# First norm from feature tiles summed on GpSimd, first projection tiles evacuated unscaled, memory norm moved into the key projection

## The chip, the cores and the metric

One core of a Trainium2 chip runs the whole kernel. The metric is the device time in microseconds of one execution; a run's median over several executions is compared. The engines are named as in the profile: PE (TensorE matmul), PEld (its weight load), DVE (VectorE), ACT (ScalarE), POOL (GpSimd), SP (SyncE, which here only issues DMAs).

## The reference

A decoder trunk of two layers on 256 positions of 2048 features, with 256 memory tokens. Only its beginning matters here:

```
mem_n = rms_norm(mem, norm_mem)
hn = rms_norm(h, norm_mix[0])            # y = x * rsqrt(mean(x*x) + eps) * g
z = hn @ w_in                            # (256 x 2048) @ (2048 x 4096)
gate_b, gate_c, xa, u = split(z)         # u: the last 1024 columns, input of the S5 branch
ya = gate_b * causal_dwconv(gate_c * xa, conv_w)
ys = s5_branch(u, ...)                   # a scan over positions
h = h + concat(ya, ys) @ w_out
# then, in each layer: cross attention into mem_n
k, v = split(mem_n @ w_kv, 2)            # w_kv of each of the two layers
```

Behind it come cross attention, a gated MLP with a short convolution, a layer with sliding-window attention, again cross attention and MLP, and a final norm.

## The kernel before

Features lie on the 128 partitions and the 256 positions along the free dimension, so an activation is 16 tiles (`KT`) of 128 x 256. All products are float32 in three passes: operand and weight are each split into a rounded high part and the rest. `split_gain` does it for an activation, with the norm's gain on the way: ACT writes the high part (L67) and DVE the rest (L68). `wload` does it for a weight block: SP issues its DMA into one of three `raw` buffers (L82), ACT writes `hi` (L90), DVE writes `lo` (L91); `hi` and `lo` have four buffers of 128 x 1024 each, two weight tiles' worth. `mm_hi` multiplies `hi` with both parts of the operand (128 x 512 moving columns at once at L105, or two times 256 at L102 and L103 with `one=True`), `mm_lo` multiplies `lo` with the high part (L110). `add_halves` adds the two halves of a PSUM bank (ACT copy L160, DVE add L161). PSUM has two pools of four banks each, `pp` (for `gemm`) and `pm` (`bank()`).

A norm's factor depends on the position alone, so it can be applied after the product. In later layers its sums come from `stat_add` on each new residual tile: ACT squares the tile (L174), POOL adds the squares up (L172); `stat_col` sums over partitions with a one-column matmul (L186), `rsqrt_col` takes the inverse root with an initial guess and three Newton steps on DVE, and `stat_bc` spreads it over partitions with a diagonal matrix (L225) and a matmul (L227) as `rbc`.

The first norm is done in another way. `even_mixer` starts with the eight weight tiles of `u`, numbers 24 to 31 of `ev_w_in`. `first_tiles` computes tiles 0 to 3 of them together while x and the weights arrive in pieces, k-tile by k-tile. `tok_col` loads x a second time with the positions on the partitions (`x_tok`, two DMAs on ACT's queue, released by a copy that waits for `h[10]`), and one ACT square for each half, with its sum along the row (L201), gives the column of sums. Tiles 4 and 5 go to banks of the pool `pm`; the broadcast is issued behind tile 4. Then the memory's sums are taken in the same way from `mem_tok`, and `memT` is loaded with the features on the partitions. Only then are tiles 0 to 5 evacuated by `evac_u`, which multiplies with `rbc`. `gemm` does tiles 6 and 7, with half of the sixteen `split_gain` of the memory behind each. Last come the memory's broadcast and `load_consts`, nine small constant loads on SP.

`x_tok`, `mem_tok`, `memT` and the states of S5's odd groups take turns in one buffer (tag `S`, one slot).

`mem_kv` then computes keys (`xa_k`, 16 tiles) and values (`xa_v`) of the memory for both layers; `after`, called behind each tile, takes steps of the generator `s5`, so that the S5 branch (DVE, ACT, a few matmuls) is spread over this time. The gates' 24 tiles follow, and the output projection. A key is stored unscaled, and scaled with the memory's broadcast when the cross attention loads it; a value is scaled with the column `mcol` when it is evacuated.

The order of each engine's queue is fixed when the kernel is built: a planner orders the instructions by its own costs, with the program's order as priority, so that later work is put into what it takes for gaps (S5's exponential, `vexp`, L347 and on, is an example). On the chip each queue is then followed in that order.

## Time and profile before

| | us |
|---|---|
| median of 3 runs | 2846.25 |
| lowest and highest | 2845.36, 2848.18 |
| the profiled execution | 2847.27 |
| its span, first to last instruction | 2845.5 |
| PE busy in the span | 2805.7 |
| DVE, ACT, POOL busy | 1952.9, 1566.1, 345.4 |

The profile is of one execution; its span is 1.8 us shorter than its time. All times inside it are counted from the span's start. PE's row says 99% busy, as an average over the whole kernel: the page's slices show the first of 40 at 7 tenths and nearly all others at 9 or more. A timeline row gives start, duration, engine, line, operation, out<-in, shapes, count, and in brackets the idle time of its engine before it and what ended it.

### The profile page before, as it was taken

What the parts mean: (1) busy time and instruction counts of PE and PEld (TensorE: products, weight loads), DVE (VectorE), ACT (ScalarE), POOL (GpSimd) and SP (SyncE); (2) the same over time, 40 slices, a digit from 0 to 9 for tenths busy, and PEclk for the clock granted to TensorE, in tenths of its full rate; (3) what the DMA queues carried; (4) which work ended last, traced back from release to release, by engine and by line L of the source; (5) the groups of instructions that cost most, each with busy time, mean ns of one, the idle gap of its engine ahead of it and who ended that gap; (6) DMA issues with size and microseconds to landing.
All of it is one profiled execution on the core that took longest, in us unless ns stands there. A gap on an engine that the chain in (4) does not pass through costs nothing.

```text
span 2845.5 us, 43900 instructions
## 1 busy us (share of the span) xinstructions
PE 2805.7 (99%) x17155; PEld 2492.1 (88%) x17155; DVE 1952.9 (69%) x3171; ACT 1566.1 (55%) x2509; POOL 345.4 (12%) x382
## 2 busy tenths in 40 slices
PE   7999999999999999999999999999999999999998
PEld 6988989998998888888888888889888888888887
DVE  5878697866766666666666778776666666666666
ACT  5766766644654544545545566655555455454454
POOL 0000000001001311202102310000122012021121
PEclk8999999999999999999999999999999999999999
DMA  7555555555555545555455554455455454654544
GB/s 283 204 201 189 206 191 205 210 179 181 206 188 182 189 171 210 184 185 197 170 207 184 179 193 154 154 208 185 165 188 195 165 207 171 213 189 166 208 170 142
DMA packets 90081, 538.83 MB, mean 189 GB/s; under 512 B 10672, under 2 KB 17168, under 8 KB 38672
## 3 DMA queue, kind: packets, MB, share of 16 engines
q1 hardware_dynamic: 86080, 520.47, 52.1%
q10 hardware_dynamic: 3792, 15.55, 1.4%
q8 instruction: 134, 2.20, 0.3%
q14 instruction: 75, 0.61, 0.1%
HBM read 525.45 MB, written 10.53 MB: 188 GB/s over the span
## 4 chain that ended last, share of the span: by engine, by line
PE 93%; DVE 3%; DMA 2%; ACT 1%; issue 1%; SPq 0%; POOL 0%; DVEq 0%; ACTq 0%; POOLq 0%
PE ps L105 49%; PE ps L110 28%; PE ps L102 3%; PE ps L103 3%; PE ps L326 2%; PE ps L327 2%; PE ps L331 2%; DVE lo L91 1%; PE m L856 1%; DMA raw<-in_ev_u 1%; PE m L762 1%; ACT stmp L496 1%; ACT hi L90 0%; DMA s5p<-in_s5p 0%; PE m L748 0%
## 5 line engine op out<-in xcount | busy, mean ns | idle before, releaser
L91 DVE TENSOR_TENSOR lo<-raw,hi 128x1024 fp32r<-128x1024 f32 (+2 forms) x1033 | 1202.2, 1185 | 414.4 <-ACT hi L90 161.6
L105 PE MATMUL ps<-op,hi 128*128 128x512 f32 x6069 | 1466.6, 392 | 6.5 <-DVE rcol L212 5.4
L90 ACT CAST hi<-raw 128x1024 fp32r<-128x1024 f32 (+2 forms) x1033 | 1002.1, 983 | 825.1 <-PE ps L105 695.1
L105 PEld LDWEIGHTS ps<-op,hi 128*128 128x128 f32 x6069 | 1114.3, 189 | 225.5 <-ACT hi L90 5.6
L110 PEld LDWEIGHTS ps<-op,lo 128*128 128x128 f32 x6976 | 897.4, 191 | 37.8 <-DVE lo L91 6.1
L110 PE MATMUL ps<-op,lo 128*128 128x256 f32 x6976 | 918.2, 283 | 4.8 <-DVE lo L91 4.8
L102 PE MATMUL ps<-op,hi 128*128 128x256 f32 x907 | 223.2, 286 | 6.2 <-ACT hi L90 6.1
L172 POOL TENSOR_TENSOR acc<-acc,t 128x256 f32<-128x256 f32 x84 | 77.0, 917 | 1229.1 <-ACT t L174 1229.1
L103 PE MATMUL ps<-op,hi 128*128 128x256 f32 x907 | 221.5, 284 | 0.0
L102 PEld LDWEIGHTS ps<-op,hi 128*128 128x128 f32 x907 | 174.8, 193 | 9.4 <-ACT hi L90 7.8
L103 PEld LDWEIGHTS ps<-op,hi 128*128 128x128 f32 x907 | 174.9, 193 | 0.1
L160 ACT COPY t<-ps 128x256 f32<-128x256 f32 x232 | 85.9, 371 | 150.6 <-PE ps L110 149.7
L893 POOL TENSOR_TENSOR t<-t,rbc 128x256 f32<-128x256 f32 x88 | 68.8, 781 | 749.1 <-DVE t L161 721.2
L896 DVE SCALAR_TENSOR_TENSOR t<-t,ff_conv 128x255 f32<-128x255 f32 x88 | 43.0, 488 | 141.8 <-ACT t L895 141.8
L899 POOL TENSOR_TENSOR t<-t,rbc 128x256 f32<-128x256 f32 x88 | 109.2, 1241 | 216.4 <-ACT t L898 216.4
L496 ACT ACTIVATE stmp<-S,s_pw 128x256 f32<-128x256 f32 (+3 forms) x256 | 118.0, 525 | 27.7 <-DVE S L503 24.1
L68 DVE SCALAR_TENSOR_TENSOR op<-h,gains,op 128x256 fp32r<-128x256 f32 x96 | 67.8, 713 | 86.6 <-ACT op L67 86.4
L75 DVE TENSOR_TENSOR op<-t,op 128x256 fp32r<-128x256 f32 x104 | 43.9, 425 | 116.8 <-ACT op L74 116.7
L326 PE MATMUL ps<-hi,op 128*128 128x512 f32 x256 | 101.2, 395 | 2.2 <-ACT hi L90 2.1
L327 PE MATMUL ps<-hi,op 128*128 128x512 f32 x256 | 99.9, 390 | 0.0
L161 DVE TENSOR_TENSOR t<-ps,t 128x256 f32<-128x256 f32 x232 | 96.4, 416 | 0.0
L905 POOL TENSOR_TENSOR t<-t 128x256 f32<-128x256 f32 x88 | 67.0, 762 | 135.0 <-DVE t L161 134.7
(219 smaller groups left out, 1727.9 us busy)
## 6 DMA issues: line engine op xcount, KB each, us to landing
raw<-in_ff_gate SPq DMA_DIRECT2D x88, 1024.0 KB, 4.8
raw<-in_ff_up SPq DMA_DIRECT2D x88, 1024.0 KB, 4.8
raw<-in_ff_down SPq DMA_DIRECT2D x128, 704.0 KB, 4.0
raw<-in_xa_k SPq DMA_DIRECT2D x32, 1024.0 KB, 5.1
raw<-in_xa_v SPq DMA_DIRECT2D x32, 1024.0 KB, 4.9
raw<-in_xa_q SPq DMA_DIRECT2D x32, 1024.0 KB, 4.8
raw<-in_xa_o SPq DMA_DIRECT2D x32, 1024.0 KB, 4.8
raw<-in_ev_w_in SPq DMA_DIRECT2D x28, 1024.0 KB, 4.9
```

The costliest lines, as they stand in the source:

```text
L90: nc.scalar.copy(hi, s)
L91: nc.vector.tensor_tensor(lo, s, hi.bitcast(F32), op=ALU.subtract)
L102: nc.tensor.matmul(ps[:, :T], lhsT=hi, rhs=o[:, :T], start=k == 0, stop=False)
L103: nc.tensor.matmul(ps[:, :T], lhsT=hi, rhs=o[:, T:], start=False, stop=False)
L105: nc.tensor.matmul(ps, lhsT=hi, rhs=o, start=k == 0, stop=False)
L110: self.nc.tensor.matmul(ps[:, :T], lhsT=w[k][1], rhs=ops[k][:, :T], start=False, stop=k == K - 1)
L160: self.nc.scalar.copy(t, ps[:, T:])
L161: self.nc.vector.tensor_tensor(out, ps[:, :T], t, op=ALU.add)
L326: nc.tensor.matmul(ps[b], lhsT=o[:, b * P:(b + 1) * P], rhs=w[j][0], start=k == 0, stop=False)
L327: nc.tensor.matmul(ps[b], lhsT=o[:, T + b * P:T + (b + 1) * P], rhs=w[j][0], start=False, stop=False)
L496: nc.scalar.activation(tmp[:, x, :, p - p0, :], at(0, both, p), AF.Copy, scale=pw[:, x, k, 8 * b + p:8 * b + p + 1])
L899: nc.gpsimd.tensor_tensor(y, y, self.rbc, op=ALU.mult)
```

## The change

- `tok_col` and the input `x_tok` go. `first_tiles` calls `stat_begin`, and `stat_add` on each k-tile of x, four k-tiles behind its split; `stat_col` follows behind tile 4 and `stat_bc` behind tile 5.
- Tiles 0 to 3 are evacuated at once and unscaled into their `u` buffers; tiles 4 to 7 all go through `gemm` and the pool `pp`, and are evacuated unscaled. `scale_u` multiplies the `u` tiles with `rbc` in place, six of them behind tile 5 and the others each behind its own tile.
- `memT` is loaded on SP's queue, one half behind tile 4 and one behind tile 5; the memory's splits stay behind tiles 6 and 7.
- The memory's norm moves into the first layer's key projection: `mem_tok` is loaded on SP behind key tile 2, its halves are squared behind tiles 5 and 6, `rsqrt_col` and `load_consts` follow behind tile 8, the broadcast behind tile 10.

```diff
@@ -188,19 +188,6 @@
                 nc.tensor.matmul(ps[:, b:b + 1], lhsT=self.sq[:, c], rhs=self.ones[:, :1], start=False, stop=True)
         return self.rsqrt_col(ps[:, :2], tag)
 
-    def tok_col(self, src, S, tag, behind=None):
-
-
-        nc = self.nc
-        if behind is not None:
-            nc.scalar.copy(S[:, :, 0], behind)
-        ss = self.smp.tile([P, 2], F32, name="ss", tag="ss")
-        for b in range(2):
-            nc.scalar.dma_start(S[:, b, :], src[:, b, :])
-        for b in range(2):
-            nc.scalar.activation(S[:, b, :], S[:, b, :], AF.Square, accum_out=ss[:, b:b + 1])
-        return self.rsqrt_col(ss, tag)
-
     def rsqrt_col(self, ms, tag):
         nc = self.nc
         v = self.smp.tile([P, 2], F32, name="v", tag="rs_v")
@@ -258,18 +245,24 @@
     def first_tiles(self, load_x, xs):
 
         ps = [self.pp.tile([P, 512], F32, name="ps", tag="ps") for _ in range(4)]
+        self.stat_begin()
+        lag = 4
         k = 0
         for step in (1, 1, 2, 2, 2, 4, 4):
             load_x(k, k + step)
             w = self.wload(self.I["ev_u0"][:, k:k + step, :], step, 512)
             for j in range(step):
                 xs.append(self.split_gain(self.h[k + j], self.gain(G_MIX, k + j)))
+                if k + j >= lag:
+                    self.stat_add(self.h[k + j - lag])
                 for n in range(4):
                     self.nc.tensor.matmul(ps[n], lhsT=w[j][0][:, n * P:(n + 1) * P], rhs=xs[k + j], start=k + j == 0, stop=False)
             for j in range(step):
                 for n in range(4):
                     self.nc.tensor.matmul(ps[n][:, :T], lhsT=w[j][1][:, n * P:(n + 1) * P], rhs=xs[k + j][:, :T], start=False, stop=k + j == KT - 1)
             k += step
+        for k in range(KT - lag, KT):
+            self.stat_add(self.h[k])
         return ps
 
     def load_consts(self):
@@ -302,7 +295,7 @@
         return evac, nxt
 
 
-    def mem_kv(self, l, kvp, after):
+    def mem_kv(self, l, kvp, after_k, after):
         nc = self.nc
         kv = self.dp.tile([4, P, 2048], F32, name=f"kv{l}")
         cur = {}
@@ -314,7 +307,7 @@
             nc.scalar.copy(cur["k"][:, n % 4, :], ps[:, :T])
             if n % 4 == 3:
                 nc.scalar.dma_start(kv[n // 4][:, :1024], cur["k"].rearrange("p a b -> p (a b)"))
-        self.gemm(lambda n: self.I["xa_k"][l, n], range(16), self.memop, KT, evac, after=after, one=True)
+        self.gemm(lambda n: self.I["xa_k"][l, n], range(16), self.memop, KT, evac, after=after_k, one=True)
         for c in range(4):
             ps = [self.pp.tile([P, 512], F32, name="ps", tag="ps") for _ in range(2)]
             for q in range(4):
@@ -552,36 +545,65 @@
             u, ya, ys = [], [], []
 
             def evac_u(n, ps):
-                z = self.t1()
-                self.add_halves(z, ps)
+
                 w = pool.tile([P, T], F32, name=f"u{n}", tag=f"u{n}")
-                nc.vector.tensor_tensor(w, z, rbc, op=ALU.mult)
+                self.add_halves(w, ps)
                 u.append(w)
+
+            def scale_u(ns):
+                for n in ns:
+                    nc.vector.tensor_tensor(u[n], u[n], rbc, op=ALU.mult)
+            place = lambda shape: pool.tile(shape, F32, name="S", tag="S")
             ps = self.first_tiles(load_x, xs)
-            place = lambda shape: pool.tile(shape, F32, name="S", tag="S")
-            self.tok_col(self.I["x_tok"], place([P, 2, D]), "h", self.h[10][:, :2])
-            for n in range(4, 6):
-                ps.append(self.bank())
-                self.mm(ps[n], self.wload(win(24 + n), KT, P), xs, 0, KT, KT)
+            for n in range(4):
+                evac_u(n, ps[n])
+            mem = place([P, KT, T])
+
+            def load_mem(c):
+                nc.sync.dma_start(mem[:, 8 * c:8 * c + 8, :], self.I["memT"][:, 8 * c:8 * c + 8, :])
+            self.memop = []
+
+            def mem_step(k0, k1):
+                for k in range(k0, k1):
+                    self.memop.append(self.split_gain(mem[:, k, :], self.gain(G_MEM, k)))
+
+            def after_u(n):
+                nonlocal rbc
                 if n == 4:
+                    self.stat_col()
+                    load_mem(0)
+                elif n == 5:
                     rbc, _ = self.stat_bc()
+                    load_mem(1)
+                    scale_u(range(0, 6))
+                elif n == 6:
+                    mem_step(0, 8)
+                    scale_u((6,))
+                else:
+                    scale_u((7,))
+                    mem_step(8, 16)
+            rbc = None
+            self.gemm(lambda n: win(24 + n), range(4, 8), xs, KT, evac_u, after=after_u)
             r2 = self.smp.tile([P, T], F32, name="r2", tag="r2", bufs=1)
             nc.vector.tensor_tensor(r2, rbc, rbc, op=ALU.mult)
-            self.mcol = self.tok_col(self.I["mem_tok"], place([P, 2, D]), "mem")
-            mem = place([P, KT, T])
-            for c in range(2):
-                nc.scalar.dma_start(mem[:, 8 * c:8 * c + 8, :], self.I["memT"][:, 8 * c:8 * c + 8, :])
-            for n in range(6):
-                evac_u(n, ps[n])
-            self.memop = []
-
-            def mem_step(i):
-                for k in range(8 * i, 8 * (i + 1)):
-                    self.memop.append(self.split_gain(mem[:, k, :], self.gain(G_MEM, k)))
-            self.gemm(lambda n: win(24 + n), range(6, 8), xs, KT, evac_u, after=lambda n: mem_step(n - 6))
-            self.rcol = self.mcol
-            self.mrbc, _ = self.stat_bc("mem")
-            self.load_consts()
+
+
+            mt = {}
+
+            def mem_norm(n):
+                if n == 2:
+                    mt["S"] = place([P, 2, D])
+                    mt["ss"] = self.smp.tile([P, 2], F32, name="ss", tag="ss")
+                    for b in range(2):
+                        nc.sync.dma_start(mt["S"][:, b, :], self.I["mem_tok"][:, b, :])
+                elif n in (5, 6):
+                    b = n - 5
+                    nc.scalar.activation(mt["S"][:, b, :], mt["S"][:, b, :], AF.Square, accum_out=mt["ss"][:, b:b + 1])
+                elif n == 8:
+                    self.mcol = self.rsqrt_col(mt["ss"], "mem")
+                    self.load_consts()
+                elif n == 10:
+                    self.mrbc, _ = self.stat_bc("mem")
 
             bg = self.s5(pool, u, ys)
             st = {"left": 0.0}
@@ -595,7 +617,10 @@
                         return
                     st["left"] -= c
 
-            self.kv = [self.mem_kv(l, pool, after) for l in range(2)]
+            def after_k(n):
+                mem_norm(n)
+                after(n)
+            self.kv = [self.mem_kv(l, pool, after if l else after_k, after) for l in range(2)]
             gc = {}
 
             def evac_gate(n, ps):
@@ -998,7 +1023,6 @@
     A = {}
     A["xT"] = _cols(g["x"][0].T.reshape(D, T).T).transpose(0, 2, 1)
     A["memT"] = _cols(g["mem"][0]).transpose(0, 2, 1)
-    A["x_tok"] = g["x"][0].reshape(2, P, D).transpose(1, 0, 2)
     A["mem_tok"] = g["mem"][0].reshape(2, P, D).transpose(1, 0, 2)
     A["gains"] = _cols(np.concatenate([g["norm_mix"], g["norm_xattn"], g["norm_ffn"], g["norm_final"][None], g["norm_mem"][None]]))
     A["ev_w_in"] = _tiles(g["ev_w_in"][0], P)
```

## Rows read from the trace of the kernel before

**Rows 1.** Part 1 of the page: busy us, share of the span, instructions.

```profile
PE 2805.7 (99%) x17155; PEld 2492.1 (88%) x17155; DVE 1952.9 (69%) x3171; ACT 1566.1 (55%) x2509; POOL 345.4 (12%) x382
```

**Rows 2.** Windows: length, PE, PEld, DVE, ACT, POOL busy; granted clock; DMA share, GB/s.

```profile
5.20:32.42 27.22, 24.89 (x128) 21.02 (x128) 15.71 (x24) 15.96 (x26) 0.00 (x0) 0.94 0.99 372
32.42:36.24 3.82, 0.00 (x1) 0.00 (x1) 0.82 (x5) 2.99 (x4) 0.00 (x0) 0.81 0.68 214
36.24:44.66 8.42, 8.42 (x34) 7.04 (x35) 5.85 (x14) 2.79 (x3) 0.00 (x0) 0.68 0.75 249
44.66:50.61 5.95, 5.95 (x34) 5.05 (x32) 0.43 (x1) 3.08 (x4) 0.00 (x0) 1.00 1.00 421
50.61:56.02 5.41, 0.01 (x2) 0.04 (x1) 3.01 (x19) 3.99 (x7) 0.00 (x0) 0.93 0.84 283
56.02:68.57 12.55, 10.07 (x32) 8.35 (x33) 12.07 (x65) 6.90 (x15) 0.00 (x0) 0.64 0.26 97
68.57:76.19 7.62, 6.25 (x33) 5.02 (x33) 7.62 (x18) 5.28 (x11) 0.00 (x0) 0.97 0.32 125
```

**Rows 3.** Timeline of PE, lo passes of two neighbouring key tiles.

```profile
80.97 2.08 PE L110 MATMUL ps<-op,lo 128*128 128x256 f32 x16
...
86.73 2.08 PE L110 MATMUL ps<-op,lo 128*128 128x256 f32 x16
```

**Rows 4.** Timeline of PE in the input projection.

```profile
10.87 3.69 PE L268 MATMUL ps<-op,hi 128*128 128x512 f32 x8 [2.25 <-ACT hi L90]
...
30.34 2.08 PE L271 MATMUL ps<-op,lo 128*128 128x256 f32 x16
...
73.67 1.21 PE L110 MATMUL ps<-op,lo 128*128 128x256 f32 x8 [1.11 <-DVE lo L91]
```

**Rows 5.** Timeline of ACT, the second square of x_tok.

```profile
33.25 1.91 ACT L201 ACTIVATE S<-S 128x2048 f32<-128x2048 f32 x1 [3.53 <-DMA S<-in_x_tok]
```

**Rows 6.** Timeline of DVE ahead of tile 6.

```profile
52.63 0.18 DVE L347 TENSOR_SCALAR s5p<-s5p 128x32 f32<-128x32 f32 x1 [6.73 <-DMA s5p<-in_s5p]
...
55.45 0.42 DVE L161 TENSOR_TENSOR t<-ps,t 128x256 f32<-128x256 f32 x1
```

**Rows 7.** DMA issues of 0 to 90 us: count, KB each, median us to landing.

```profile
raw<-in_ev_u SPq DMA_DIRECT2D x2, 1024.0 KB, 9.2
...
S<-in_memT ACTq DMA_DIRECT2D x2, 1024.0 KB, 6.2
...
s5p<-in_s5p SPq DMA_DIRECT2D x1, 48.0 KB, 11.0
```

**Rows 8.** By line: duration in ns (min/median/max), first and last start.

```profile
L172 POOL TENSOR_TENSOR acc<-acc,t x84: 734/747/1827, 624.5 to 2827.6; 128x256 f32<-128x256 f32 x84
...
L174 ACT ACTIVATE t<-h x90: 407/407/419, 624.0 to 2830.5; 128x256 f32<-128x256 f32 x90
...
L68 DVE SCALAR_TENSOR_TENSOR op<-h,gains,op x16: 478/480/487, 3.9 to 28.8; 128x256 fp32r<-128x256 f32 x16
```

**Rows 9.** Timeline of PE, the first broadcast.

```profile
44.44 0.59 PE L227 MATMUL m<-t,ones 128*128 128x256 f32 x2
```

**Rows 10.** Timeline of DVE and POOL where they meet, in later layers.

```profile
630.41 0.74 DVE L68 SCALAR_TENSOR_TENSOR op<-h,gains,op 128x256 fp32r<-128x256 f32 x1 [1.62 <-ACT op L67]
...
1109.95 1.33 POOL L899 TENSOR_TENSOR t<-t,rbc 128x256 f32<-128x256 f32 x1 [2.48 <-ACT t L898]
...
1109.46 2.90 DVE L91 TENSOR_TENSOR lo<-raw,hi 128x1024 fp32r<-128x1024 f32 x2 [0.17 <-PE ps L110]
...
1115.03 2.36 DVE L91 TENSOR_TENSOR lo<-raw,hi 128x1024 fp32r<-128x1024 f32 x2 [0.55 <-PE ps L110]
```

**Rows 11.** Windows of the key and value projections, columns as in the first windows.

```profile
80.00:120.00 40.00, 40.00 (x365) 39.47 (x364) 32.91 (x93) 27.33 (x49) 0.00 (x0) 1.00 0.66 239
...
160.00:200.00 40.00, 36.48 (x220) 30.59 (x219) 32.63 (x42) 30.11 (x55) 0.00 (x0) 1.00 0.56 199
```

**Rows 12.** Timeline of DVE, the last addition of S5's scan.

```profile
547.94 0.41 DVE L503 TENSOR_TENSOR S<-S,stmp 128x254 f32<-128x254 f32 x1
```

## Prediction

> **What bounds the kernel now.** I first read the page's head: the span is 2845.5 us and PE is busy in 99% of it [rows 1]. Away from the edges there is nothing to gain but fewer matmuls, and the change removes none. It touches the start, so I next cut the start into stretches at the borders of the eight tiles of the S5 input projection [rows 2]. The reader should compare PE's busy time with the length of each stretch, and look at the granted clock.
>
> One weight tile of 16 k-tiles has its price in the key projection, where PE runs without a gap: the lo passes of neighbouring tiles start at 80.97 and 86.73, so 5.76 us a tile [rows 3]. The same columns stream in the input projection, so eight tiles should take 8 x 5.76 = 46.1 us. They take from 5.20 to 76.19, 71.0 us. The excess is 24.9 us, and the stretches give it away piece by piece:
>
> - tiles 0 to 3: 27.22 - 23.04 = 4.2
> - nothing on PE: 3.8
> - tile 4: 8.42 - 5.76 = 2.7, at a granted clock of 0.68
> - tile 5: 0.2
> - nothing on PE: 5.4
> - tile 6: 12.55 - 5.76 = 6.8, at 0.64
> - tile 7: 7.62 - 5.76 = 1.9.
>
> Next come the waits that made these gaps. The 4.2 is mostly one wait of 2.25 us at 10.87, for a weight block and its cast [rows 4]; the matmuls behind it are slow (8 take 3.69 us, where tile 5's 16 and its lo pass together take 5.95). The 3.8 is ACT: its second token-order square stands 3.53 us for the second half of x_tok, and the weight casts of tile 4 stand behind it in ACT's order [rows 5]. The 5.4 is DVE and the banks: tile 6 needs a bank of tile 0, tile 0's add runs at 55.45, and it stands on DVE behind S5's exponential, which had waited 6.73 us for s5p [rows 6]. In tile 6 the lo casts are behind S5's small operations, on DVE again (12.07 busy of 12.55). After either gap the granted clock is near 0.65: the gap is paid about one and a half times.
>
> **The change, part by part.**
>
> *x_tok removed.* Gone are 2 MB of DMA, two squares of 1.91 us, and the wait of 3.53. The last 1 MB block of first-tile weights took about 9 us to land [rows 7], partly beside x_tok; but PE did not stand in that stretch beyond the wait at 10.87, so I give tiles 0 to 3 no gain and keep 4.2. Tile 4's weights no longer wait for x_tok: the 3.8 and tile 4's 2.7 go.
>
> *Sums by feature tile.* 16 squares on ACT at 0.407 us are 6.5 us, against 3.8 for the two squares they replace; the ACT time is there (15.96 busy of 27.22 in the first stretch). POOL gets 15 additions at a median of 0.747 [rows 8], 11.2 us in a stretch of 27 in which POOL does nothing now [rows 2]. The last four squares and sums come behind the last splits, some 4 us; the column sums stand only after tile 4, so this is covered by tile 4's 5.76. On PE the column sums are two one-column matmuls and the broadcast is about 0.6 [rows 9]; I put down 1.1 together.
>
> What the sums may cost is DVE time. The trace shows additions meeting DVE elsewhere: a split, which reads two SBUF inputs and takes 0.48 in the first tiles [rows 8], took 0.74 beside an addition at 630.41; two lo casts that take 2.36 took 2.90 beside a POOL product, which itself took 1.33 [rows 10]. So one meeting costs DVE 0.26 to 0.54. Fifteen meetings cost 3.9 to 8.1; nothing if they fall into DVE's idle time (15.71 busy of 27.22). I take 3.9, since half of these meetings are with splits and DVE has idle time for some.
>
> The Trainium skill (SBUF — State Buffer, "SBUF: two separate sides") says that GpSimd and a DVE operation with two SBUF inputs hold one port pair by turns, for a whole instruction. The 1.33 of the POOL row bears this out. By it, an addition that goes first could hold DVE for all of its length: the first rival below has this case worked out, 7.0 us gained in place of 14.3.
>
> *Early unscaled evacuation.* The adds and scalings are as many as before (8 and 8), the scaling in place. Tiles 0 to 3 leave PSUM without rbc, so tile 6 has no wait for an old bank: the 5.4 goes. But tile 4 now takes a bank of the four where before it had a spare one. Tiles 0 to 3 end within 0.4 us of each other; then come a copy (about as long as a square, 0.41 [rows 8]) and an add (0.42) [rows 6] before tile 4 may start: at least 0.85 with the hand-overs. If a cast on ACT and a lo cast on DVE stand in front, 1.18 each [rows 10], it is 3.2. I take 1.5: casts for tile 4 can be done ahead, but the squares are in the same order. A wait of 1.11 at 73.67 was not followed by slow matmuls (8 lo matmuls in 1.21), the one of 2.25 was [rows 4]; I add nothing for the clock.
>
> *Memory loads and splits.* memT (2 MB) goes to SP's queue behind weight loads, without waiting for mem_tok's squares. Needed by K tile 0 are 6 + 4 + 2 MB and some key weights, about 14 MB: at the 372 GB/s of the first stretch 38 us, well before 60. The 16 splits are needed at the same place as before. DVE's list from 32.4 to K tile 0: lo casts of 4 tiles at 2.36 (9.4), 16 splits at 0.48 (7.7), 8 adds and 8 scalings at 0.42 (6.7), and an estimated 3 for the Newton steps, diagonals and r2, all of them shorter rows than these: 26.8 us in 29.6. It fits with 2.8 to spare, against S5's small operations and POOL's meetings. That is tight, hence the 3.9 above on the path.
>
> *Memory norm in the key projection.* Two mem_tok loads, two squares (1.91 each), twelve tiny DVE steps and a diagonal, a broadcast that was at K tile 0 before too, and nine constant loads on SP. I cost these at nothing: the cover is ACT's 12.7 idle us of 80 to 120 and DVE's 7.1 [rows 11], and weight buffers filled ahead. Without it: 3.8 on ACT, or 6.5 if a gap of 3.8 on PE brings tile 4's clock loss again. S5's setup that ran before 76 moves into this stretch as well. S5 itself has room: its scan ends at 547.9 [rows 12], and the output projection that needs it has its second tile summed at 624.5 [rows 8], so it starts at about 610.
>
> **The sum.** K tile 0 starts at 5.20 + 23.0 + 4.2 + 1.5 + 23.0 + 1.1 + 3.9 = 61.9, in place of 76.2: 14.3 us earlier. Everything behind is PE-bound and shifts along. The profiled execution took 2847.27 (span 2845.5 and 1.8 around it), so it would take 2833.0; against the median of the runs, 1.0 lower, 2832.
>
> **The rivals.**
>
> *DVE becomes the bound.* POOL's additions block DVE for whole instructions, 15 x 0.747 = 11.2 on the path in place of 3.9. For it: DVE is busy 12.07 of 12.55 and 7.62 of 7.62 in the last two stretches. Against: eleven of the additions fall where DVE has 11.5 idle us [rows 2]. It gives 14.3 - 7.3 = 7.0 gained, 2839.
>
> *A late load on an in-order queue.* memT's second half stands on SP behind a weight load that waits for a raw buffer, or S5's exponential again stands on DVE for s5p (11 us to land [rows 7]). If memT issues only when tile 7 is nearly done, at 57, it lands 6.2 us later [rows 7] and 16 splits of 0.48 follow (7.7): K tile 0 at 71, with a clock loss of 2.7 at 73. Gain 3, 2843, no measurable change. For it: s5p did this before. Against: the raw buffers run three tiles ahead, and memT has nothing else to wait for.
>
> *The key projection becomes DVE-bound.* S5's setup (about 8 us: DVE's 15.1 busy from 50.61 to 68.57, less two lo casts, some seven adds and scalings and the Newton steps), the memory norm's steps (3) and the first scan meet in a stretch where DVE has 7.1 idle in 40. If the lo casts fall behind, PE stands, and a gap such as the one of 3.8 costs 6.5 with its clock loss. Three gaps take the whole gain (19.5 against 14.3); from four on it is slower: 26.0 - 14.3 = 11.7, 2858. For it: 3.5 us of PE are idle between 160 and 200 now [rows 11]. Against: the four lo buffers are two tiles' worth, and no such gap stands between 80 and 120 now, with DVE at 32.91 of 40.
>
> **Chances and range.** The forecast 0.70; DVE bound by POOL 0.13; late load 0.10; slower 0.07. The forecast's own ends: no POOL cost and the short bank wait give 14.3 + 3.9 + 0.65 = 18.9, 2827; 8.1 and 3.2 in their place give 8.4, 2838. The first rival must be taken in and part of the second left out: 2826 to 2841. About 0.2% (5.7 us) can be told from no change here. Faster: the forecast and most of the first rival, 0.81; same: the second and the rest, 0.11; slower 0.08.
>
> **What would show it.** Right: PE busy without a gap over 1.5 us from about 33 to the key projection at a granted clock near 1.0; K tile 0's first matmul at 60 to 64; no ACT wait for a token-order load before it. Wrong: a DVE row of 1.2 us grown to 1.7 or more beside POOL in the first 32 us and PE waiting for lo; K tile 0 waiting for a split behind memT; new gaps between 80 and 200 that were not there, or the clock under 0.9 there.

## The result, and the profile after

The changed kernel takes 2825.55 us (median of 4 runs, 2824.97 to 2825.75), the kernel before 2846.53 beside it: a ratio of 0.9926, 95% interval 0.9911 to 0.9942. The sign was as forecast, and the gaps at the start went as it said; the size was not as forecast. The gain is 21.0 us, the forecast was 14.3, and the time lies 0.45 below the range's lower end.

The profiled execution took 2825.51, its span is 2823.7, 21.8 shorter than before. Part 1 of its page, as in [rows 1]:

```profile
PE 2797.2 (99%) x17159; PEld 2487.4 (88%) x17159; DVE 1956.9 (69%) x3171; ACT 1566.1 (55%) x2520; POOL 358.2 (13%) x397
```

PE is busy 8.5 us less than before for four more instructions, so 8.5 of the 21.8 is time in which PE ran slowly, and the rest is time in which it stood. Where both were says the start, cut at the borders of the tiles as in [rows 2] (first window: tiles 0 to 3; then the gap; then tiles 4 to 7; then K tile 0 up to its lo pass; the last two are later stretches):

```profile
4.91:32.56 27.65, 24.13 (x130) 20.71 (x130) 23.73 (x27) 21.04 (x43) 12.85 (x15) 1.00 0.97 359
32.56:33.80 1.24, 0.51 (x6) 0.42 (x4) 1.24 (x5) 1.24 (x5) 0.00 (x0) 1.00 1.07 416
33.80:39.52 5.72, 5.72 (x33) 5.02 (x33) 5.72 (x19) 5.35 (x11) 0.00 (x0) 1.00 0.66 249
39.52:45.08 5.56, 5.56 (x34) 4.91 (x33) 5.33 (x15) 5.21 (x9) 0.00 (x0) 1.00 0.67 239
45.08:51.14 6.06, 6.06 (x37) 5.23 (x35) 6.06 (x14) 4.72 (x8) 0.00 (x0) 1.00 0.57 192
51.14:56.70 5.56, 5.56 (x34) 4.91 (x33) 5.35 (x11) 2.48 (x3) 0.00 (x0) 1.00 0.81 305
...
56.70:60.54 3.84, 3.84 (x34) 3.84 (x33) 3.63 (x12) 2.04 (x3) 0.00 (x0) 1.00 1.01 425
...
60.00:100.00 40.00, 40.00 (x365) 39.46 (x365) 37.22 (x151) 30.92 (x52) 0.00 (x0) 1.00 0.73 262
...
100.00:160.00 60.00, 57.45 (x450) 55.48 (x450) 52.18 (x93) 37.96 (x70) 0.00 (x0) 1.00 0.46 161
```

From 33.80 on PE's busy time equals each stretch, at a granted clock of 1.00: the two gaps of [rows 2] and the clock of 0.64 to 0.68 behind them are gone, and eight tiles take 51.8 where they took 71.0. DVE is nearly full there too (22.46 of the 22.90 from 33.80 to 56.70), and does not hold PE up. The timeline of PE at the same places:

```profile
11.51 2.09 PE L259 MATMUL ps<-op,hi 128*128 128x512 f32 x8 [2.38 <-ACT hi L90]
...
32.56 0.50 PE L186 MATMUL m<-ones,acc 128*128 128x1 f32 x4
...
33.80 3.96 PE L105 MATMUL ps<-op,hi 128*128 128x512 f32 x16 [0.74 <-DVE u L161]
...
60.54 2.08 PE L110 MATMUL ps<-op,lo 128*128 128x256 f32 x16
```

The wait for a weight block in the first tiles is as before (2.38 here, 2.25 in [rows 4]); the new wait for a bank is 0.74 long; K tile 0's lo pass starts at 60.54 instead of 80.97 [rows 3]. From there to the end of the span it is 2763.2 in place of 2764.5.

The splits of x by line (columns as in [rows 8]):

```profile
L68 DVE SCALAR_TENSOR_TENSOR op<-h,gains,op x16: 482/958/967, 4.0 to 27.1; 128x256 fp32r<-128x256 f32 x16
```

The timeline of DVE, then POOL, where they meet:

```profile
18.69 3.58 DVE L68 SCALAR_TENSOR_TENSOR op<-h,gains,op 128x256 fp32r<-128x256 f32 x4
...
18.24 3.74 POOL L172 TENSOR_TENSOR acc<-acc,t 128x256 f32<-128x256 f32 x4 [0.89 <-ACT t L174]
```

Four splits take 3.58 us while four additions run from 18.24 to 21.98: the median split has grown from 0.480 to 0.958. The meetings are real and as dear as feared. What they cost the kernel is the question of the first experiments.

### The profile page after: what moved, and what is told of

Read it like the earlier page. It is cut to its first block, busy times and chain, and to the rows that moved or that the text cites. A ratio compares the mean times of both kernels' runs of the same rounds, so it can differ in the third digit from the quotient of the medians.

```text
span 2823.7 us, 43952 instructions
## 1 busy us (share of the span) xinstructions
PE 2797.2 (99%) x17159; PEld 2487.4 (88%) x17159; DVE 1956.9 (69%) x3171; ACT 1566.1 (55%) x2520; POOL 358.2 (13%) x397
## 4 chain that ended last, share of the span: by engine, by line
PE 93%; DVE 3%; ACT 2%; DMA 1%; issue 0%; SPq 0%; POOL 0%; DVEq 0%; ACTq 0%; POOLq 0%
PE ps L105 49%; PE ps L110 28%; PE ps L102 3%; PE ps L103 2%; PE ps L319 2%; PE ps L320 2%; PE ps L324 2%; DVE lo L91 1%; PE m L881 1%; ACT stmp L489 1%; PE m L787 1%; DVE stmp L493 1%; DMA kv<-kst 1%; ACT hi L90 0%; DVE S L494 0%
## 5 line engine op out<-in xcount | busy, mean ns | idle before, releaser
L172 POOL TENSOR_TENSOR acc<-acc,t 128x256 f32<-128x256 f32 x98 | 89.4, 912 | 1194.7 <-ACT t L174 1190.7
```

What stands on the lines that cost most here:

```text
L172: nc.gpsimd.tensor_tensor(self.acc, self.acc, self.sq, op=ALU.add)
```

## The experiments

Each kernel is told by three numbers: when K tile 0's lo pass starts (what the start took), the rest from there to the end of the span, and the median with its ratio to the kernel before in the same comparison. The first two are of one profiled execution each. The changed kernel and v1 to v4 have the same instructions in the same order on every engine up to about 66 us, and yet their lo pass starts at 59.35 to 60.59: a difference of 1 us in that column says nothing by itself.

| | lo pass of K tile 0 | rest | median | ratio, 95% |
|---|---|---|---|---|
| before | 80.97 | 2764.5 | 2846.5 | |
| after | 60.54 | 2763.2 | 2825.55 | 0.9926 (0.9911 to 0.9942) |
| e1_more_pool | 66.40 | 2763.8 | 2830.53 | 0.9945 (0.9930 to 0.9960) |
| e2_no_pool | 59.68 | 2770.4 | 2831.28 | 0.9947 (0.9930 to 0.9963) |
| e3_dve_sum | 60.05 | 2764.4 | 2826.65 | 0.9931 (0.9916 to 0.9946) |
| e6_small_pool | 59.78 | 2763.3 | 2824.89 | 0.9924 (0.9912 to 0.9937) |
| u1_x_tok | 65.75 | 2767.7 | 2834.81 | 0.9958 (0.9942 to 0.9975) |
| u2_late_evac | 63.99 | 2768.4 | 2833.96 | 0.9957 (0.9942 to 0.9972) |
| u3_mem_early | 66.84 | 2769.7 | 2838.91 | 0.9976 (0.9967 to 0.9986) |
| s3_mem_only | 69.21 | 2764.4 | 2835.60 | 0.9962 (0.9950 to 0.9975) |
| e4_dve_3 | 60.32 | 2765.5 | 2827.49 | 0.9933 (0.9918 to 0.9947) |
| e5_dve_6 | 60.38 | 2768.5 | 2830.83 | 0.9945 (0.9931 to 0.9960) |
| v1_kst_halves | 60.59 | 2755.8 | 2817.99 | 0.9899 (0.9884 to 0.9914) |
| v2_s5_17 | 60.34 | 2760.9 | 2822.55 | 0.9916 (0.9902 to 0.9929) |
| v3_s5_23 | 59.35 | 2766.0 | 2827.82 | 0.9934 (0.9921 to 0.9948) |
| v4_halves_s5_17 | 59.59 | 2757.1 | 2818.96 | 0.9905 (0.9889 to 0.9920) |

### What do the meetings of POOL and DVE cost?

**Eight more additions** on POOL in the first tiles, into a spare tile that nothing reads:

```diff
+        acc2 = self.smp.tile([P, T], F32, name="r2", tag="r2", bufs=1)
...
                 if k + j >= lag:
                     self.stat_add(self.h[k + j - lag])
+                if k + j < 8:
+                    self.nc.gpsimd.tensor_tensor(acc2, self.h[k + j], self.h[k + j] if k + j == 0 else acc2, op=ALU.add)
```

> The changed kernel with 8 further additions on POOL in the first 20 us (h tiles summed into a spare tile, not used). In the changed kernel a split beside an addition took 0.88 in place of 0.48-0.41, so a meeting costs DVE about 0.45. Theory (slack): in the first stretch DVE waits for weights anyway, so K tile 0 stays within 0.7 us of 56.7 and the time within 1 us of 2825.6. Rival (path, as predicted): each meeting lands on the path, 8 x 0.26 to 0.48 = 2 to 4 us later, 2828 to 2830.

K tile 0 came 5.9 us later, more than either theory gave eight additions. Its timeline, DVE and PE:

```profile
30.09 5.70 DVE L91 TENSOR_TENSOR lo<-raw,hi 128x1024 fp32r<-128x1024 f32 x4
...
33.58 1.22 PE L265 MATMUL ps<-op,lo 128*128 128x256 f32 x8 [0.46 <-DVE lo L91]
...
36.98 6.62 PE L105 MATMUL ps<-op,hi 128*128 128x512 f32 x16 [1.84 <-DVE u L161]
```

The window of its tile 4:

```profile
36.98:45.35 8.37, 8.37 (x33) 6.99 (x33) 6.14 (x19) 4.25 (x8) 0.00 (x0) 0.65 0.65 239
```

The reader sees the first rival's mechanism: lo casts behind the additions (5.70 for four, where after they take 4.62), PE waiting for them, the first tiles ending at 34.64 (2.1 later), the wait for a bank 1.84 in place of 0.74, and behind it tile 4 at a granted clock of 0.65: 8.37 in place of 5.72, 2.65 more. So 3.2 of the 5.9 arise in front of tile 4 and the rest in it; the four executions of this kernel took 2828.70 to 2831.98, the profiled one is the longest, and the slow tile need not be in all of them. The first tiles have room for 15 additions, not for 23.

**The additions left out** (the sums are then those of the first k-tile's squares alone), **and the additions on DVE** in the place of POOL:

```diff
-        if self.accn > 1:
+        if self.accn > 1 and not self.first:
             nc.gpsimd.tensor_tensor(self.acc, self.acc, self.sq, op=ALU.add)
```

```diff
-            nc.gpsimd.tensor_tensor(self.acc, self.acc, self.sq, op=ALU.add)
+            (nc.vector if self.first else nc.gpsimd).tensor_tensor(self.acc, self.acc, self.sq, op=ALU.add)
```

> The changed kernel without POOL's 15 additions in the first norm: the squares are made, but only the first one is used for the norm, so the sums are left out. Theory (slack): DVE's splits fall back to 0.48 and DVE is some 6 us less busy in the first 33 us, but K tile 0 starts within 0.7 us of 56.7 and the time is within 1 us of 2825.6. Rival (path): 3.9 to 6.7 us earlier, about 2819 to 2822.

> The changed kernel with the 15 additions of the first norm on DVE in place of POOL, 0.34 to 0.42 each, 5 to 6 us of DVE. Theory (slack): as the meetings cost DVE about as much (14 x 0.45), K tile 0 moves by less than 1 us and the time stays within 1.5 us of 2825.6. Rival (GpSimd takes load off DVE): the lo casts of the last first-tile block come later and PE waits, 3 us or more.

Without the additions K tile 0 comes 0.9 earlier, and yet the kernel is 5.7 slower, which neither theory said: the rest is 7.2 longer. With the additions on DVE nothing changes that can be told. The timeline of the kernel without additions, ACT and then PE:

```profile
148.59 0.93 ACT L491 ACTIVATE stmp<-S,s_pw 128x126 f32<-128x126 f32 x2 [12.48 <-DVE S L498]
...
126.60 2.35 PE L110 MATMUL ps<-op,lo 128*128 128x256 f32 x16 [0.78 <-DVE lo L91]
...
149.74 3.17 PE L110 MATMUL ps<-op,lo 128*128 128x256 f32 x16 [2.09 <-DVE lo L91]
```

The same of the changed kernel:

```profile
144.17 0.94 ACT L489 ACTIVATE stmp<-S,s_pw 128x126 f32<-128x126 f32 x2 [10.63 <-DVE S L496]
...
145.32 2.35 PE L110 MATMUL ps<-op,lo 128*128 128x256 f32 x16 [1.35 <-DVE lo L91]
...
148.84 0.39 PE L102 MATMUL ps<-op,hi 128*128 128x256 f32 x1 [1.17 <-ACT hi L90]
```

Some 90 us behind the edit, ACT stands 10 to 12 us for a step of S5's first scan on DVE, with weight casts queued behind it. In the changed kernel PE then waits twice, without the additions four times for lo casts (0.78, 1.11, 1.38 and 2.09). POOL does nothing in that stretch in either kernel: it is the order that the planner wrote that differs, and it differs in the first tiles too, where the column sums of the first norm, which no longer wait for POOL, run on PE at 9.13 in place of 32.56. So e2 does not measure the meetings.

**The additions cut short**: each adds 8 of the 256 columns (`cols` is 8 in the first norm and 256 behind it; the other columns keep the first k-tile's squares alone). The order on every engine is then the same, instruction for instruction, as in the changed kernel.

```diff
-            nc.gpsimd.tensor_tensor(self.acc, self.acc, self.sq, op=ALU.add)
+            c = slice(0, self.cols); nc.gpsimd.tensor_tensor(self.acc[:, c], self.acc[:, c], self.sq[:, c], op=ALU.add)
```

> The changed kernel with POOL's 15 additions of the first norm cut to 8 of 256 columns (the other columns' sums are left out), so short that DVE meets them hardly. All engines have the same instructions in the same order as in the changed kernel, so nothing but the length of the additions differs. Theory (the meetings are covered): DVE some 6 us less busy up to 33 us, K tile 0 at most 1 us earlier than 56.7, the stretch behind it as in the changed kernel, time 2824.5 to 2826. Rival (the meetings are on the path, and the run without additions hid it by another order behind): 3 to 6 us earlier, 2819.5 to 2822.5.

Its splits by line:

```profile
L68 DVE SCALAR_TENSOR_TENSOR op<-h,gains,op x16: 477/480/485, 3.9 to 24.5; 128x256 fp32r<-128x256 f32 x16
```

PE's timeline behind the wait for a weight block, at tile 4 and at K tile 0:

```profile
11.41 2.08 PE L259 MATMUL ps<-op,hi 128*128 128x512 f32 x8 [2.16 <-ACT hi L90]
...
33.04 3.96 PE L105 MATMUL ps<-op,hi 128*128 128x512 f32 x16 [0.28 <-DVE u L161]
...
59.78 2.08 PE L110 MATMUL ps<-op,lo 128*128 128x256 f32 x16
```

A window over the first tiles, of this kernel and then of the changed one, with a part of it:

```profile
4.90:33.00 28.10, 24.71 (x134) 21.17 (x133) 19.37 (x30) 21.94 (x46) 4.39 (x15) 1.00 0.96 371
```

```profile
4.90:33.00 28.10, 24.58 (x134) 21.14 (x133) 24.18 (x28) 21.48 (x44) 12.85 (x15) 1.00 0.97 360
...
11.49:32.56 21.07, 19.91 (x112) 17.37 (x113) 21.07 (x22) 17.12 (x35) 11.07 (x13) 1.00 0.97 379
```

This is the clean measure. The meetings make DVE 4.8 us busier (24.18 against 19.37). K tile 0 is 0.76 earlier without them, but the weight block's arrival alone shifts it by more than that from kernel to kernel. Counted from the first matmul behind that wait, tile 4 starts 22.29 later in the changed kernel (11.51 to 33.80), 22.29 to 22.32 in v1 to v4, and 21.63 here (11.41 to 33.04): the path is 0.66 longer by the meetings. The medians also differ by 0.66, though the executions of the two kernels overlap. The other four microseconds fall into time in which DVE would have stood. That room is used up: from 11.49 on DVE is busy for all of 21.07 us in the changed kernel. So the eight additions more of e1 go onto the path.

### Which part brought the gain?

**x_tok and its squares put back**, in place of the sums by feature tile:

```diff
-                if k + j >= lag:
-                    self.stat_add(self.h[k + j - lag])
...
             ps = self.first_tiles(load_x, xs)
+            self.tok_col(self.I["x_tok"], place([P, 2, D]), "h", self.h[10][:, :2])
```

> The changed kernel with the first norm from x_tok again (two loads on ACT's queue released by h[10], two squares on ACT), all else as changed. Theory (as predicted): the second square stands on ACT for its load, tile 4's casts and the evacuations of tiles 0 to 3 stand behind it: 3.8 plus 2.7 of clock, 6.5 us later, 2832; somewhat more because memT has to wait for the shared buffer. Rival (other work hides it, since tile 4 now waits for a bank too): within 2 us of 2825.6.

K tile 0 is 5.2 later, where the first theory said 6.5. ACT and PE in its timeline, the first row to be set beside [rows 5]:

```profile
32.90 1.91 ACT L201 ACTIVATE S<-S 128x2048 f32<-128x2048 f32 x1 [3.55 <-DMA S<-in_x_tok]
...
36.98 5.98 PE L105 MATMUL ps<-op,hi 128*128 128x512 f32 x16 [6.39 <-ACT hi L90]
```

**Tiles 0 to 5 evacuated late and scaled**, behind the broadcast:

```diff
-            for n in range(4):
-                evac_u(n, ps[n])
...
+            for n in range(4, 6):
+                ps.append(self.bank())
+                self.mm(ps[n], self.wload(win(24 + n), KT, P), xs, 0, KT, KT)
+                after_u(n)
+            for n in range(6):
+                evac_u(n, ps[n])
```

> The changed kernel with tiles 0 to 5 evacuated only when the broadcast is there, scaled on the way, and tiles 4 and 5 in the other PSUM pool, as before; sums by feature tile and the memory norm as changed. Theory (the late broadcast holds the banks only a little): the broadcast is there at 47.5, tile 0's bank at about 48.5, tile 6 could start at 44 to 45: 3 to 4 us later plus perhaps 2.7 of clock, less 1.2 for the bank wait of tile 4 that goes: 2827 to 2831. Rival (early evacuation carries the gain of the second gap): 8 us or more later, 2834 and up.

K tile 0 is 3.5 later, as the first theory said; the time is nearer to the rival's 2834, since the rest is 5.2 longer. PE waits 2.03 for the broadcast's diagonal and 0.80 for tile 0's add, and tile 6's hi pass takes 5.31, where tile 7's takes 3.82 in the changed kernel.

```profile
46.06 0.67 PE L214 MATMUL m<-t,ones 128*128 128x256 f32 x2 [2.03 <-DVE t L212]
...
47.52 5.31 PE L105 MATMUL ps<-op,hi 128*128 128x512 f32 x16 [0.80 <-DVE t L161]
```

**The memory's sums put back** in front of the key projection, with memT on ACT's queue behind them:

```diff
-                    load_mem(0)
...
-                    load_mem(1)
                     scale_u(range(0, 6))
+                    self.mcol = self.tok_col(self.I["mem_tok"], place([P, 2, D]), "mem")
+                    mem = place([P, KT, T])
+                    for c in range(2):
+                        nc.scalar.dma_start(mem[:, 8 * c:8 * c + 8, :], self.I["memT"][:, 8 * c:8 * c + 8, :])
```

> The changed kernel with the memory norm back ahead of the key projection: mem_tok into the shared buffer, squared on ACT, then memT into the same buffer, both on ACT's queue as before. Theory (the late memory loads made the second gap): ACT stands for mem_tok, memT lands after that, and K tile 0 waits for its splits: 8 to 14 us later than 56.7, 2834 to 2840. Rival (the gap was the banks alone, and early evacuation cured it): within 3 us of 2825.6.

It loses 13.4 us, inside the 2834 to 2840 of the first theory, but that is luck: at K tile 0 it loses 6.3 and not 8 to 14, and the rest is 6.5 longer. A part of the 6.3 is something that the theories did not speak of. With no x_tok in its buffer, the first half of mem_tok's load has nothing to wait for, and it runs at the very start, beside the first weights (first two rows; then DVE and PE ahead of tile 6, and the lo passes of K tile 0, whose second half follows at 68.04, and of K tile 1):

```profile
1.25 0.39 ACTq L199 DMA_DIRECT2D S<-in_mem_tok  x1
...
8.17 1.81 PE L272 MATMUL ps<-op,hi 128*128 128x512 f32 x4 [2.93 <-DVE op L68]
...
48.81 0.18 DVE L353 TENSOR_SCALAR s5p<-s5p 128x32 f32<-128x32 f32 x1 [2.53 <-DMA s5p<-in_s5p]
...
50.54 3.93 PE L105 MATMUL ps<-op,hi 128*128 128x512 f32 x16 [0.41 <-ACT hi L90]
...
66.84 1.12 PE L110 MATMUL ps<-op,lo 128*128 128x256 f32 x8
...
72.12 2.08 PE L110 MATMUL ps<-op,lo 128*128 128x256 f32 x16
```

PE's first matmul of the projection is at 8.17 in place of 4.91. So this run can't price the part cleanly. It does show tile 6: S5's exponential begins ahead of it and waits for s5p, as in [rows 6], but PE waits only 0.41 for it, for a weight cast and not for a bank, since the adds of tiles 0 to 3 had run from 35.89 on. The other way round there is no late first matmul: **the kernel before with the memory part alone** (memT on SP behind tiles 4 and 5, the norm in the key projection by the change's own `mem_norm`; x_tok and the late evacuation stay).

```diff
+                nc.sync.dma_start(mem[:, 8 * (n - 4):8 * (n - 4) + 8, :], self.I["memT"][:, 8 * (n - 4):8 * (n - 4) + 8, :])
...
-            self.mcol = self.tok_col(self.I["mem_tok"], place([P, 2, D]), "mem")
...
-            self.rcol = self.mcol
-            self.mrbc, _ = self.stat_bc("mem")
-            self.load_consts()
+            def mem_norm(n):
...
```

> The kernel before with the memory part of the change alone: memT loaded on SP behind tiles 4 and 5, the memory norm in the key projection; x_tok and the late, scaled evacuation stay. Theory (the gap in front of tile 6 and its slow passes came from ACT and DVE standing for memory loads and S5's setup): the gap of 3.8 in front of tile 4 stays, the 5.4 and most of tile 6's 6.8 go: K tile 0 some 10 us earlier than 76.2, time 2834 to 2838. Rival (they came from the late evacuation, as predicted): K tile 0 at most 3 us earlier, 2843 to 2847.

PE's timeline at tile 4, the broadcast, and the lo passes of tiles 5 and 6, and DVE's at S5's exponential:

```profile
35.92 5.78 PE L105 MATMUL m<-op,hi 128*128 128x512 f32 x16 [4.90 <-ACT hi L90]
...
46.52 1.06 PE L227 MATMUL m<-t,ones 128*128 128x256 f32 x2 [2.91 <-DVE t L225]
...
52.32 2.08 PE L110 MATMUL m<-op,lo 128*128 128x256 f32 x16
...
57.89 2.08 PE L110 MATMUL ps<-op,lo 128*128 128x256 f32 x16
...
67.94 0.18 DVE L347 TENSOR_SCALAR s5p<-s5p 128x32 f32<-128x32 f32 x1
```

K tile 0 is at 69.21: the memory part alone brings 11.8 of the 20.4 us. The x_tok wait in front of tile 4 is still there (4.90), and so is one for the broadcast (2.91); the wait in front of tile 6 is gone (the two lo passes are 5.57 apart), although tiles 0 to 3 leave their banks only from 46.8 to 50.5, around the broadcast. S5's exponential, at 52.63 with its 6.73 us of waiting in [rows 6], now comes at 67.94, behind the input projection, and waits for nothing. With u1 and u2 the account closes, 11.8 + 5.2 + 3.5 = 20.5 against 20.4, closer than the spread of that column lets one expect. It is the account of one order, the memory first and the others on top. In the other order the two others bring 14.1 without the memory (80.97 to 66.84 in u3), and the memory 6.3 on top of them. What lies between 11.8 and 6.3, 5.5, is about the gap of 5.4 in front of tile 6, which either the memory's move (s3) or the early evacuation (u3) takes away; as u3 starts late, that equality is rough.

### What does the rest hang on?

**Unused additions on DVE** behind each of tiles 4 to 7, three in e4 (as below) and six in e5, 12 and 24 in all (24 x 0.42 = 10 us of DVE):

```diff
+                for _ in range(3):
+                    nc.vector.tensor_tensor(z2, u[n], u[n], op=ALU.add)
```

> The changed kernel with 12 further additions of 128x256 on DVE behind tiles 4 to 7 (unused results), 4.1 us of DVE between 40 and 60. It asks how much room DVE has ahead of the key projection. Theory (the predicted list of 26.8 us in 29.6 was too long and DVE has room): K tile 0 and the first two key tiles move by less than 1 us, 2825 to 2827. Rival (DVE is just full there): about 4 us later, 2830.

> The same with 24 further additions on DVE, 8.2 us. Theory (room of some 4 us, the rest pushes S5's setup into the key projection): up to 4 us later, 2826 to 2830. Rival (DVE just full): about 8 us later plus a clock loss, 2834 to 2837.

K tile 0 does not move, though DVE was 98% busy there and e5's additions stand between 40.9 and 65.0. S5's preparation gives way, and the price comes in the rest: 2.3 and 5.3 more, somewhat over the first theory of each. In e5 PE waits four times for lo casts between 127 and 151 (0.92, 1.09, 1.38, 2.09), as in e2.

**S5 handed out in other portions.** `after` lets the S5 generator go forward by S5_US = 2.0 of the planner's microseconds behind each key tile. With 1.7 and 2.3, nothing in front of the key projection is edited:

```diff
-    S5_US, S5_V, S5_G = 2.0, 2.1, 1.8
+    S5_US, S5_V, S5_G = 1.7, 2.1, 1.8
```

> The changed kernel with 1.7 in place of 2.0 units of S5 work per key tile; all work stays. Up to K tile 0 nothing differs. Theory (the stretch from K tile 0 to the end depends on where the first scan's small steps meet the key tiles, and that alone moved it by up to 7 us between the runs): K tile 0 within 0.3 us of 56.7, and the stretch behind it differs by 1 to 6 us, either way. Rival (that stretch depends on DVE's load at the start, not on the order): the stretch stays within 1 us of 2763.2 from the low pass of K tile 0 to the end, the time within 1 us of 2825.6.

> As the run with 1.7 units, with 2.3. Theory (order): K tile 0 within 0.3 us of 56.7, the stretch behind it differs by 1 to 6 us, probably longer, as the first scan then falls in a denser stretch. Rival: within 1 us of the changed kernel.

The rest moves by -2.3 and +2.8 us: where S5's steps stand among the casts is worth several microseconds by itself.

**A stall that both kernels have.** In the changed kernel, ACT then PE:

```profile
265.82 0.37 ACT L307 COPY kst<-ps 128x256 f32<-128x256 f32 x1 [4.15 <-DMA kv<-kst]
...
269.97 0.58 PE L102 MATMUL ps<-op,hi 128*128 128x256 f32 x1 [4.10 <-ACT hi L90]
```

A key's evacuation waits for the store of the values from the same buffer, and the weight casts wait behind it. Before it is there too, 4.07 long at 291.29. With two buffers of half the size:

```diff
-            if n % 4 == 0:
-                cur["k"] = kvp.tile([P, 4, T], F32, name="kst", tag="kst")
+            if n % 2 == 0:
+                cur["k"] = kvp.tile([P, 2, T], F32, name="kst", tag="kst", bufs=2)
...
-            if n % 4 == 3:
-                nc.scalar.dma_start(kv[n // 4][:, :1024], cur["k"].rearrange("p a b -> p (a b)"))
+            if n % 2 == 1:
+                c0 = 512 * (n % 4 // 2)
+                nc.scalar.dma_start(kv[n // 4][:, c0:c0 + 512], cur["k"].rearrange("p a b -> p (a b)"))
```

(and the values' `vs` likewise, one half at a time)

> The changed kernel with the staging buffer of keys and values split in two halves that take turns, so that a copy needn't wait for the write of the block before. In the changed kernel PE stands 4.1 us near 270 because ACT stands for such a write. Theory: that stall shrinks to 1 us or less, 3 to 4 us gained, 2822. Rival: the halves change the planned order and another stall takes its place, within 1.5 us of 2825.6 or worse.

```profile
266.32 0.39 PE L102 MATMUL ps<-op,hi 128*128 128x256 f32 x1 [0.42 <-ACT hi L90]
```

2817.99 (2817.10 to 2818.34), 7.6 us under the changed kernel, where the theory said 3 to 4: the stall of 4.10 is 0.42, and the lo wait of 1.35 at 145 is gone with the new order. These are 5.0 of the 7.6; where the others lie was not followed. This is the fastest of all. **Both together** (halves and 1.7) bring no more:

> The changed kernel with the staging buffer in halves (2818.0 alone) and 1.7 units of S5 work per key tile (2822.6 alone, 3.0 under the changed kernel). Theory (two independent stalls): the gains add, 2815. Rival (both took away the same stall of 4.1 us near 270, the one by the buffer, the other by another order): no more than the halves alone, 2817 to 2820.

2818.96, within 1 us of the halves alone, as the rival said: with 1.7 alone the same wait is already down to 0.84, at 265.74.

## Why the prediction was right in kind and short in size

The forecast put K tile 0's start at 61.9 in the profile; it is at 56.70, 5.2 earlier. Another 2.3 came behind it. By the terms of its sum:

- **Tiles 0 to 3, 5.20 + 23.0 + 4.2:** they end at 32.56, forecast 32.4. Right, with the old weight wait in them, as assumed.
- **The wait for a bank, 1.5, and the column sums, 0.5 of the 1.1:** together 1.24 (0.74 and 0.50), 0.76 less. The copies and adds did run one behind the other, and no cast stood in front of them. e1 shows the bound above: its wait is 1.84, and there the clock fell.
- **Four tiles at 5.76, and 0.6 for the broadcast:** 22.90 in place of 23.6. The price came from the key projection, whose hi passes are two of 256 columns; these tiles' hi pass is one of 512, and three windows of four show 5.56 to 5.72. A term of the right kind read from a neighbouring form, 0.7 off.
- **POOL's additions, 3.9 on the path:** this is the step that failed, and the largest of the differences. A meeting costs more than the 0.26 it was sized with (a split 0.48 more), DVE's busy time grew by 4.8, and yet tile 4 starts only 0.66 later for it (22.29 against 21.63 in e6, counted from the weight wait; 0.46 of that is the wait for a bank), and this is already in the two terms above. The prediction had counted DVE's idle time, 11.5 us in [rows 2], and then charged 15 meetings to the path all the same; some four of the 4.8 fitted into it.
- **"Everything behind is PE-bound and shifts along":** wrong by 2.3; without them the time would lie inside the range. 0.94 lies in K tile 0 itself: before, 4.78 passed from the end of tile 7 to its lo pass [rows 2, 3], with the memory's broadcast in between; now it is 3.84. The other 1.3 is in the rest, and is less than the 2.8 by which the executions of the kernel before differ. But the rest runs from 2755.8 to 2770.4 among these kernels. It hangs, among other things, on where S5's steps stand in the order (v2 and v3 edit nothing else), and an edit far ahead can shift that (e2, e4, e5). The prediction's own lowest case, 2827, held the start's terms alone; a spread for the rest was missing from the range.

**The place of the gain.** The forecast gave the 5.4 us gap and tile 6's slowness to the early evacuation, and cost the move of the memory's norm at nothing. That its steps cost nothing in the key projection is right: PE is busy 40.00 of 40.00 from 60 to 100, as in the first of [rows 11], and 57.45 of the 60 behind it, where the 60 us behind 120 before had 57.39. But the move also brings a gain of its own, which the forecast had at nothing: alone it brings 11.8 at K tile 0 and takes the wait in front of tile 6 with it (s3). The forecast's way is there as well: in u3, with the memory in front and the early evacuation, the chain of [rows 6] begins as before and tile 6 waits for no bank. So the gap goes by either part, and with both in, each shows what the other leaves: 3.5 for the evacuation, 6.3 for the memory (with u3's late start in it); x_tok is worth 5.2, forecast 6.5. In s3 the exponential no longer stands in front of tile 6, with the memory's loads and squares out of the way. That the planner saw a gap behind mem_tok and filled it is the likely reason; its costs were not varied, so this is argued only.

**The rivals.** The first, DVE held by POOL, has its mechanism confirmed and its price refuted: the Trainium skill (SBUF — State Buffer, "SBUF: two separate sides") has a two-input DVE operation and a GpSimd operation take one port pair by turns for whole instructions, and splits of 0.96 beside additions point the same way, though they are 0.48 longer and not the 0.75 of a whole addition. But a DVE instruction that takes twice as long costs only what exceeds DVE's slack: 0.66 with 15 additions, 3.2 more with 23, and then 2.65 by the clock. The late load did not come: tile 7 and K tile 0 run without a wait. The DVE-bound key projection did not come either: PE stands there as long as before, and the runs that made it worse (e2, e5) lost 5 to 7 us, not the 26 of the rival's price.

**The undoings** lose 9.3 (x_tok), 8.4 (evacuation) and 13.4 us (memory), 31 together against a gain of 21. They do not add up since they also lengthen the rest, by 4.5, 5.2 and 6.5. At K tile 0 they lose 15.0 together, less than the 20.4, as the gap in front of tile 6 stays away, or small, while one of two parts is in. A part of the longer rest is seen at S5's first scan: between 130 and 160 PE waits four times in u2 (1.10, 1.37, 2.08 and 1.17), where it waits twice in the changed kernel (1.35 and 1.17). Where the remainder lies was not followed.

## What to carry to other kernels

When two engines share something, price the meeting and then look for who has slack: a cost belongs on the path only where it exceeds the idle time of the engine that pays it, and one run with the shared work made small but its order kept (e6) measures that cleanly, where leaving it out (e2) also reorders the program and can even show the wrong sign. In a kernel whose order is planned as a whole, give a forecast a term for the far end: edits in the first 60 us moved the remaining 2760 by several microseconds. Split a change both ways, undoing each part and doing one alone: an undone part may meet a machine that is not the one before, as mem_tok's load did when its buffer stood empty, and two parts may take away the same gap, so that each looks small when the other is in.

## What the runs showed of the hardware that was not expected

- A split of 128x256 on DVE takes 0.480 us alone and 0.958 in the median beside POOL's additions, and these take 0.802 in the median (up to 1.389) in place of 0.747: both sides pay, DVE more.
- A wait of 0.74 us in front of tile 4 left the granted clock at 1.00 over the next 23 us; one of 1.84, with small waits for lo casts ahead of it, was followed by a tile at 0.65. The loss was 2.65 us, more than the wait itself. The length of the wait alone does not tell it: in the changed kernel eight matmuls behind a wait of 2.38 took 2.09 us, in the kernel before eight behind one of 2.25 took 3.69 [rows 4].
